# Where the SBUF tiles lie: both operands of every matrix product at whole multiples of 256 bytes

## The chip, the cores and the metric

The kernel runs on one core of one Trainium2 chip. What is measured is device time in microseconds (us) of one execution. The kernel before takes 1617.59 us (median of three runs, 1617.21 to 1617.77). The on-chip memory SBUF has 128 partitions; a tile has the same byte address in each of them, so "address" below means the byte within a partition.

## The reference

One layer of a decoder: a normalised input goes through one wide projection, then two token mixers run side by side (a three-branch attention and a retention), their outputs are gated and projected, and a two-matrix MLP follows. Sequence 1024, width 1024, MLP width 4096, all in float32. Cut to its skeleton:

```
h = rmsnorm(x)
q, kc, vc, ks, vs, kw, vw, gates, rq, rk, rv, rg, gate_a, gate_b = split(h @ w_in)
A = nsa_mixer(...)                 # compressed + selected + sliding-window attention
B = silu(rg) * retention(rq, rk, rv)
x = x + (sigmoid(gate_a) * (A @ w_proj_a) + sigmoid(gate_b) * (B @ w_proj_b)) @ w_out
x = x + square(relu(rmsnorm(x) @ w_up)) @ w_down
return rmsnorm(x)
```

## The kernel before

**How a float32 product is made.** TensorE multiplies a stationary operand (128 columns, loaded by a weight load, shown as PEld) by a moving operand of up to 512 columns that streams past it. A float32 value is split into a high part (`h`, made by a copy to float32r on ScalarE) and a low part (`l`, the difference, on VectorE). A product of two such values is three TensorE products: high by high, high by low, low by high, added up in PSUM. Every one of them goes through `mm` on line 157, so nearly all TensorE time stands on that line, and the tile names tell the products apart.

**Stages, in order of time.**

- 0 to 430 us, the wide projection and the retention. `bh`, `bl` (the two parts of the normalised, transposed input, 8 by 1024 columns) are stationary, 128 columns at a time; the weights `wh`, `wl` move, 512 columns (280 for `w_kvb`). `dense_tok` issues 24 products per token tile; every two inner steps it calls `tick`, which may put other work in between, and products of the retention and transposes stand between the token tiles.
- 430 to 790 us, attention. Scores are `QQ`, `ql` by `KKs`, `KKw`, `KKc`; probabilities are transposed and multiplied with `Vs`, `Vw`, `Vc`. Pieces of the gate products (`gps`: `wh`, `wl` stationary, `bh`, `bl` moving) are put between them, three products at a time.
- 790 to 880 us, the two mixer projections: `wh`, `wl` stationary, `Ah`, `Al`, `Bh`, `Bl` moving. The PSUM tile is shown as `mm` here too.
- 880 to 986 us, the output projection (`mmu`), 16 runs of 24 products with `bh`, `bl` stationary and the weights moving, and four transposes between the runs.
- 986 to 1302 us, the first MLP matrix (`mmu`): seven products of 12 for each of 16 weight groups (a Strassen-like scheme), `wh`, `wl` stationary, `bh`, `bl` or the forms `t2h` to `t4l` moving.
- 1302 to the end, the second MLP matrix (`mmd`): 1344 products whose two operands both come from the ring of split tiles `wh`, `wl`.

The order of TensorE's instructions is written out by hand for the whole program (`manual_schedule`, line 116); the order on the other engines follows from a scheduler with the pools' buffers.

**Where tiles lie.** A pool takes its place on a stack from the left end of SBUF or, with `side="right"`, on one from the right end, and gives it back when it closes. The tiles of a pool stand one behind the other, each rounded up to 32 bytes. In the built program the left stack begins at byte 16512 (128 past a multiple of 256), the right one ends at byte 229344 (224 past one). The first pool on the left, `cst`, holds the identity matrix (512 bytes) and five small tiles of 64, 32, 32, 64 and 32 bytes as rounded; 736 bytes in all, so that everything on the left behind it begins 96 past a multiple of 256, as far as the tiles between are multiples of 256 themselves. `cret` (2848 bytes), `cmp_m` (480 bytes), the four buffers each of `sums`, `mx` and `cf` (32 bytes each) shift what follows them further. On the right `big` (with `bh`, `bl`) ends at byte 229344. The remainders of the operands' first bytes by 256, out of the built programs of before and after:

| tiles | remainder before | after |
|---|---|---|
| `bh`, `bl`; `t2h` to `t4l`; `KKs`, `KKw`, `KKc`, `Vs`, `Vw`, `Vc`; `qt`, `qkT` | 224 | 0 |
| `wh`, `wl` in the pools `wring`, `wr4`, `wr5`, `wr7`; `Ah`, `Al`, `Bh`, `Bl`; `x1t` | 96 | 0 |
| `wh`, `wl` in `wrx` and `wr2`; the retention's `s`, `v`, `n`, `sd`; `ident` | 128 | 0 |
| `QQ`, `ql`, `pS`, `pW` | 64 | 0 |
| `ph`, `pl` | 192 | 0 |
| slices of `w_kvb` (280 columns, 1120 bytes apart) | 96, 128, 192, 224 | 0 |

All slices that are used as operands otherwise begin at multiples of 512 bytes within their tiles. Before, the products of the 790 to 880 us stage and of the last stage have both operands at 96; all other products with 512 moving columns have operands with two different remainders (224 with 96 or 128 or 64).

Of the kernel before, what the change touches and what calls it, by code (L numbers as in the profile page):

```python
# [9 lines left out]
F32 = mybir.dt.float32  # L10
F32R = mybir.dt.float32r
I32 = mybir.dt.int32
AF = mybir.ActivationFunctionType
OP = mybir.AluOpType
# [3 lines left out]
P = 128  # L18
S = 1024
D = 1024  # L20
NT = S // P
KD = D // P
# [90 lines left out]
def hybrid_block(ctx: ExitStack, tc: tile.TileContext, a: dict, out: bass.AP):  # L113
    nc = tc.nc
    V, A, G, T = nc.vector, nc.scalar, nc.gpsimd, nc.tensor
    ctx.enter_context(tc.manual_schedule(engines={mybir.EngineType.PE}))

    cst = ctx.enter_context(tc.tile_pool(name="cst", bufs=1, reuse_waits="tile"))
    dram = ctx.enter_context(tc.tile_pool(name="scr", bufs=1, space=DRAM))
    bigs = ctx.enter_context(ExitStack())  # L120
    big = bigs.enter_context(tc.tile_pool(name="big", bufs=1, side="right", reuse_waits="tile"))
    wraw = ctx.enter_context(tc.tile_pool(name="wraw", bufs=3, reuse_waits="tile"))
# [8 lines left out]

    bh = big.tile([P, KD, S], F32R, name="bh")
    bl = big.tile([P, KD, S], F32R, name="bl")
    ident = cst.tile([P, P], F32, name="ident")
    small = cst.tile([P, 16], F32, name="small")
    nhalf = cst.tile([P, 4], F32, name="nhalf")
    gcol = cst.tile([P, KD], F32, name="gcol")
    ssx = cst.tile([P, 2, NT], F32, name="ssx")
    rr = cst.tile([P, NT], F32, name="rr")
    V.memset(nhalf, -0.5)  # L140
    clock = {"t": 0, "n": 0}
    due = []
# [13 lines left out]
    def mm(o, w, m, start, stop):  # L156
        T.matmul(o, w, m, start=start, stop=stop)  # L157

    def load_raw(src, shape):
        r = wraw.tile([P, 1024], F32, name="raw", tag="raw")  # L160
        n = int(np.prod(shape))
        v = r[:, :n]
        if len(shape) == 2:
            v = v.rearrange("p (a b) -> p a b", a=shape[0])
        nc.sync.dma_start(v, src)
        return r[:, :n], n
# [6 lines left out]
    def new_slot(pool=None):  # L173
        if pool is None:
            pool = ring["pools"][ring["i"] % len(ring["pools"])]
            ring["i"] += 1
        h = pool.tile([P, 1024], F32R, name="wh", tag="wh")
        l = pool.tile([P, 1024], F32R, name="wl", tag="wl")
        return h, l

    def split_w(src, shape, eng=None, pool=None):
        r, n = load_raw(src, shape)
        h, l = new_slot(pool)
        A.activation(h[:, :n], r, AF.Copy)
        (eng or V).tensor_tensor(l[:, :n], r, h[:, :n], op=OP.subtract)  # L185
        return h, l
# [41 lines left out]
    def chunk_weights(name, n, s0=0, s1=4):  # L228
        per = 2
        W = []  # L230
        for s in range(s0, s1):
            h, l = split_w(a[name][:, s * per:(s + 1) * per, :], (per, n))
            for e in range(per):
                W.append((h[:, e * n:(e + 1) * n], l[:, e * n:(e + 1) * n]))
        return W

    with ExitStack() as es:
        psA = es.enter_context(tc.tile_pool(name="psA", bufs=2, space=PSUM, reuse_waits="tile"))
        tabs = es.enter_context(tc.tile_pool(name="tabs", bufs=1, reuse_waits="tile"))
        cret = tabs.tile([P, P + 512 + 72], F32, name="cret")  # L240
        cosr = tabs.tile([P, NT, 64], F32, name="cosr")
        sinr = tabs.tile([P, NT, 64], F32, name="sinr")
        cosn = tabs.tile([P, NT, 8], F32, name="cosn")
# [5 lines left out]
        with ExitStack() as e1:  # L249
# [150 lines left out]
            with tc.manual_schedule(engines={mybir.EngineType.PE, mybir.EngineType.Pool}):  # L400
# [9 lines left out]
                W = chunk_weights("w_r0a", 512, 0, 1)  # L410
# [24 lines left out]
            for c in range(2):  # L435
                rt = {}
                for j in range(NT):
# [21 lines left out]
                    if j == NT - 1:  # L459
                        W = chunk_weights(f"w_r{c}b", 512)  # L460
# [4 lines left out]
                for j in range(NT):  # L465
                    ps = psA.tile([P, 512], F32, name="mm", tag="mm")
                    dense_tok(ps, j, W, 0, 4)
                    if j == 0:
                        s = ret_s(0, qkT)
# [8 lines left out]
                    if j == NT - 1:  # L478
                        W = chunk_weights("w_kva" if c else "w_r1a", 512)
                    v, y = ret_v(j, ps)  # L480
                    cur = (j, c, qkT, s, v, y)
                    if j + 1 < NT:
                        qkT = qkTn
                        s = ret_s(j + 1, qkT)
# [32 lines left out]
        with ExitStack() as e2:  # L517
# [157 lines left out]
            for j in range(2, NT):  # L675
                ps = psA.tile([P, 512], F32, name="mm", tag="mm")
                dense_tok(ps, j, W)
                if j == NT - 1:
                    W = chunk_weights("w_kvb", 280)
                kva_post(j, ps)  # L680
            for j in range(NT):
# [5 lines left out]
                if j == NT - 1:  # L687
                    W = chunk_weights("w_q", 512)
                n = tmp.tile([P, 512], F32, name="n")[:, :256]
# [13 lines left out]
            for i, j in enumerate(reversed(range(NT))):  # L703
# [6 lines left out]
                n = tmp.tile([P, 512], F32, name="n")  # L710
# [56 lines left out]
    with ExitStack() as e3:  # L767
        msk = e3.enter_context(tc.tile_pool(name="msk", bufs=1, reuse_waits="tile"))
# [2 lines left out]
        psO = e3.enter_context(tc.tile_pool(name="psO", bufs=1, space=PSUM, reuse_waits="tile"))  # L771
        at = e3.enter_context(tc.tile_pool(name="at", bufs=2, reuse_waits="tile"))
        edge_m = msk.tile([P, 640], F32, name="edge_m")
        cmp_m = msk.tile([P, 120], F32, name="cmp_m")
        nc.sync.dma_start(edge_m, a["c_edge"])
        nc.sync.dma_start(cmp_m, a["c_cmp"])
        nc.sync.dma_start(gcol, a["norm_mlp"].rearrange("o (k p) -> p (o k)", p=P))
# [17 lines left out]
        def scores(qb, g, hp, u):  # L795
            QQ, ql = qs[qb, g]
            nk, nw = qb + 1, min(qb + 1, 5)
            cS, cW = nk * P, nw * P
            w0 = (nk - nw) * P
            u.update(nk=nk, nw=nw, P=[])  # L800

            def mask(c0, n, width, edge):
                if c0 + n == width:
                    return edge_m[:, 640 - n:]
                return edge_m[:, :n] if edge else edge_m[:, P:P + 1].to_broadcast([P, n])

            for i in range(2):
                h = hp * 2 + i
                sums = at.tile([P, 5], F32, name="sums", bufs=4)
                mx = at.tile([P, 5], F32, name="mx", bufs=4)  # L810
                pS = at.tile([P, 1024], F32, name="pS", bufs=PS_S)
                pW = at.tile([P, 768], F32, name="pW", bufs=PS_S)
                G.memset(pW[:, 704:], 0.0)
                for base, KK, start, width, p in ((1, KKs, 0, cS, pS), (2, KKw, w0, cW, pW)):
                    groups = []
                    for c0 in range(0, width, 512):
                        n = min(512, width - c0)
                        groups.append([(base if c0 == 0 else base + 2, KK, start + c0, n,
                                        mask(c0, n, width, base == 2), p[:, c0:c0 + n])])
                    split = len(groups) > 1  # L820
                    if base == 2:
                        tail = (0, KKc, 0, 64, cmp_m[:, 56 - 8 * qb:120 - 8 * qb], pW[:, 640:704])
                        if groups[-1][0][3] <= 448:
                            groups[-1].append(tail)
                        else:
                            groups.append([tail])
                    exps = []
                    for gi, grp in enumerate(groups):
                        ps = psS.tile([P, 512], F32, name="S")
                        off = 0  # L830
                        done = []
                        for b, K, c0, n, mk, o in grp:
                            done.append((b, ps[:, off:off + n], mk, o))
                            off += n
                        _, K, c0 = grp[0][:3]
                        mm(ps[:, :off], QQ[:, h], K[:, g, c0:c0 + off], True, False)
                        mm(ps[:, :off], ql[:, h], K[:, g, c0:c0 + off], False, True)
                        for b, sc, mk, o in done:
                            V.tensor_tensor_reduce(sc, sc, mk, -0.125, BIGPOS, OP.add, OP.min, mx[:, b:b + 1])  # L839
                            exps.append((b, sc, o))  # L840
                        if gi < len(groups) - 1:
                            yield
                    if split:
                        V.tensor_tensor(mx[:, base:base + 1], mx[:, base:base + 1], mx[:, base + 2:base + 3],
                                        op=OP.min)
                    for b, sc, o in exps:
                        m = b - 2 if b > 2 else b
                        A.activation(o, sc, AF.Exp, bias=mx[:, m:m + 1], scale=-1.0, accum_out=sums[:, b:b + 1])  # L848
                    if base == 1:
                        yield  # L850
                if cS > 512:
                    V.tensor_add(sums[:, 1:3], sums[:, 1:3], sums[:, 3:5])
                cf = at.tile([P, 3], F32, name="cf", bufs=4)
                V.reciprocal(cf, sums[:, :3])
                hd = g * 4 + hp * 2 + i
                V.tensor_mul(cf, cf, gts[:, qb, hd * 3:hd * 3 + 3])  # L856
                for b, v in ((1, pS[:, :cS]), (2, pW[:, :cW]), (0, pW[:, 640:704])):
                    G.tensor_scalar(v, v, cf[:, b:b + 1], 1.0, op0=OP.mult, op1=OP.mult)  # L858
                u["P"].append((pS, pW))
                yield  # L860
# [95 lines left out]
    with ExitStack() as e4:  # L956
# [40 lines left out]
        for i in range(8):  # L997
            h, l = pw[i]
# [56 lines left out]
    with ExitStack() as e5:  # L1055
# [40 lines left out]
        def up_first(X, ticks=False):  # L1096
            p1 = headp.tile([P, 512], F32, name="p1")
            A.activation(p1, prod(X[11], 11, ticks), AF.Copy)
            return {"p1": p1}
# [7 lines left out]
        with ExitStack() as e6:  # L1107
# [44 lines left out]
            W = out_w(0)  # L1152
            for c in range(2):
                cs = slice(c * 512, (c + 1) * 512)
                order = (0, 1, 4, 2, 5, 3, 6, 7) if c else range(NT)
                for n, j in enumerate(order):
# [4 lines left out]
                    if c == 0 and n == NT - 1:  # L1161
                        W = out_w(1)
# [71 lines left out]
        s = heads[0]  # L1234
        for p in range(16):
# [8 lines left out]
            if p < 15:  # L1244
                up_weights(p + 1, nra, nX)
                X = nX
                s = heads[1] if p == 0 else up_first(X)
# [90 lines left out]
    for step, n in enumerate((1, 2, 7, 6, 5, 4, 3)):  # L1338
# [12 lines left out]
        for i in range(4):  # L1351
            b = bank[i]
# [83 lines left out]
```

## Time and profile before

| | |
|---|---|
| median of three runs | 1617.59 us |
| the profiled execution, its own time | 1619.48 us |
| its span on the core | 1617.7 us |
| TensorE busy | 1576.0 us, 97% of the span, 7879 products |
| VectorE, ScalarE, GpSimd busy | 1070.7, 731.8, 436.5 us |
| mean granted TensorE clock | 0.991 |

The span is the time from the first to the last instruction that the hardware profiler saw. A product's duration in the trace runs from its start to its modelled end and is longer than its distance to the next product, since products are pipelined: of products that follow each other without a break, the distance from start to start is the *pace*, and it is the pace, not the duration, that adds up to time. A view of a window gives, for each engine, the time in which it was busy and the number of instructions that touch the window.

### The profile page before, as it was taken

Reading aid. Unit: us, or ns where it says so; the run is one execution under the profiler, and the core shown is the slowest. Engines: PE = TensorE matmul, PEld = TensorE weight load, DVE = VectorE, ACT = ScalarE, POOL = GpSimd, SP = SyncE. Lnnn points to the kernel's source line nnn. Section 1 sums busy time; section 2 is a strip of 40 time slices with the busy share of each in tenths; the row PEclk is TensorE's granted clock in tenths of the full one; section 3 lists DMA queues with packets and bytes.
Section 4 is the critical chain, followed back from the end, with each engine's and each line's share of the span. In section 5 each row is a group of like instructions: output and inputs, shape, how many; then the busy total and the mean of one; then the engine's idle time right before and its main releaser. Section 6 shows DMA issues by size and latency. Waiting matters only on the chain.

```text
span 1617.7 us, 22741 instructions
## 1 busy us (share of the span) xinstructions
PE 1576.0 (97%) x7879; PEld 1307.3 (81%) x7879; DVE 1070.7 (66%) x2170; ACT 731.8 (45%) x1627; POOL 436.5 (27%) x516
## 2 busy tenths in 40 slices
PE   7999999999999999999999998999999999999997
PEld 5888888887888888888788876888888878888886
DVE  4765564573777777776655367777667657885683
ACT  5454454573677766676522233222222234443442
POOL 4211010001232323333000013644555426621320
PEclk7999999999999999999999999999999999999999
DMA  6112101252111111121544322444444498674472
GB/s 213 50 36 66 52 18 43 66 182 67 49 47 34 53 46 53 47 60 60 182 144 156 109 94 74 160 144 145 152 153 150 160 332 286 207 230 126 132 269 101
DMA packets 98915, 191.83 MB, mean 119 GB/s; under 512 B 26928, under 2 KB 29360, under 8 KB 98800
## 3 DMA queue, kind: packets, MB, share of 16 engines
q1 hardware_dynamic: 98240, 188.55, 35.8%
q0 software_dynamic: 560, 1.84, 0.3%
q8 instruction: 62, 1.02, 0.3%
q14 instruction: 53, 0.43, 0.1%
HBM read 140.02 MB, written 50.33 MB: 118 GB/s over the span
## 4 chain that ended last, share of the span: by engine, by line
PE 83%; DVE 5%; ACT 4%; issue 3%; POOL 2%; DMA 2%; SPq 0%; POOLq 0%; ACTq 0%; DVEq 0%
PE mmu L157 23%; PE mm L157 20%; PE mmd L157 18%; PE gps L157 8%; PE S L157 4%; PE O L157 3%; PE pt L894 2%; PE pt L893 2%; ACT pW L848 1%; DVE S L839 1%; DVE pl L896 1%; PE pO L157 1%; PE pc L157 1%; ACT pS L848 1%; DVE wl L185 0%
## 5 line engine op out<-in xcount | busy, mean ns | idle before, releaser
L1030 DVE TENSOR_TENSOR wl<-raw,wh 128x1024 fp32r<-128x1024 f32 x121 | 182.8, 1535 | 68.5 <-ACT wh L1029 68.3
L1029 ACT ACTIVATE wh<-raw 128x1024 fp32r<-128x1024 f32 x121 | 125.2, 1056 | 217.8 <-PE mmd L157 131.3
L157 PE MATMUL mm<-wh,bh 128*128 128x512 f32 (+1 forms) x448 | 177.1, 395 | 1.0 <-ACT n L581 1.0
L157 PE MATMUL mm<-wh,bl 128*128 128x512 f32 (+1 forms) x448 | 172.7, 385 | 4.7 <-DVE bl L211 4.7
L157 PE MATMUL mmd<-wl,wh 128*128 128x512 f32 x448 | 174.6, 390 | 1.6 <-DVE wl L1030 1.6
L157 PE MATMUL mmd<-wh 128*128 128x512 f32 x448 | 174.5, 390 | 0.9 <-DVE u L1216 0.9
L157 PE MATMUL mmd<-wh,wl 128*128 128x512 f32 x448 | 174.5, 389 | 0.0
L157 PE MATMUL mm<-wl,bh 128*128 128x512 f32 (+1 forms) x448 | 172.1, 384 | 0.1
L896 DVE TENSOR_TENSOR pl<-pt,ph 128x512 fp32r<-128x512 f32 (+1 forms) x160 | 103.8, 649 | 30.2 <-ACT ph L895 27.8
L895 ACT ACTIVATE ph<-pt 128x512 fp32r<-128x512 f32 (+1 forms) x160 | 90.3, 567 | 55.0 <-PE pt L894 51.0
L839 DVE CUSTOM_DVE_ANT_0 S<-S,edge_m 128x512 f32<-128x512 f32 (+3 forms) x192 | 100.7, 530 | 14.7 <-PE S L157 12.7
L157 PE MATMUL gps<-bh,wh 128*128 128x512 f32 x256 | 108.5, 424 | 0.3 <-ACT gst L751 0.2
L858 POOL TENSOR_SCALAR pS<-pS,cf 128x1024 f32<-128x1024 f32 (+7 forms) x64 | 47.8, 748 | 220.2 <-DVE cf L856 71.4
L157 PEld LDWEIGHTS mm<-wh,bl 128*128 128x128 f32 x448 | 85.2, 190 | 22.9 <-DVE bl L211 5.7
L157 PE MATMUL mmu<-bh,wh 128*128 128x512 f32 x256 | 101.3, 396 | 0.0
L157 PE MATMUL mmu<-bl,wh 128*128 128x512 f32 x256 | 101.1, 395 | 0.0
L157 PE MATMUL mmu<-bh,wl 128*128 128x512 f32 x256 | 100.9, 394 | 0.0
L157 PE MATMUL gps<-bh,wl 128*128 128x512 f32 x256 | 100.9, 394 | 0.0
L157 PE MATMUL gps<-bl,wh 128*128 128x512 f32 x256 | 100.7, 393 | 0.0
L157 PEld LDWEIGHTS mmd<-wl,wh 128*128 128x128 f32 x448 | 84.1, 188 | 19.4 <-DVE wl L1030 2.0
L157 PEld LDWEIGHTS mmd<-wh 128*128 128x128 f32 x448 | 84.1, 188 | 18.5 <-issue 1.3
L157 PEld LDWEIGHTS mmd<-wh,wl 128*128 128x128 f32 x448 | 84.1, 188 | 17.5
(312 smaller groups left out, 3975.3 us busy)
## 6 DMA issues: line engine op xcount, KB each, us to landing
raw<-u_scr SPq DMA_DIRECT2D x56, 512.0 KB, 3.9
raw<-w_down SPq DMA_DIRECT2D x41, 512.0 KB, 4.7
raw<-w_up SPq DMA_DIRECT2D x32, 512.0 KB, 3.6
u_scr<-u SPq DMA_DIRECT2D x60, 256.0 KB, 2.3
u_scr<-s SPq DMA_DIRECT2D x45, 256.0 KB, 2.1
y<-w_down SPq DMA_DIRECT2D x16, 512.0 KB, 6.7
x<-x SPq DMA_DIRECT2D x8, 512.0 KB, 3.9
qt<-q_scr SPq DMA_DIRECT2D x32, 128.0 KB, 2.5
```

Source lines behind the costliest of these rows:

```text
L157: T.matmul(o, w, m, start=start, stop=stop)
L839: V.tensor_tensor_reduce(sc, sc, mk, -0.125, BIGPOS, OP.add, OP.min, mx[:, b:b + 1])
L848: A.activation(o, sc, AF.Exp, bias=mx[:, m:m + 1], scale=-1.0, accum_out=sums[:, b:b + 1])
L858: G.tensor_scalar(v, v, cf[:, b:b + 1], 1.0, op0=OP.mult, op1=OP.mult)
L893: T.transpose(tp[:, bi * 2], p0, ident)
L894: T.transpose(tp[:, bi * 2 + 1], p1, ident)
L895: A.activation(ph[:, :n], tp[:, :n], AF.Copy)
L896: V.tensor_sub(pl[:, :n], tp[:, :n], ph[:, :n])
L1029: A.activation(h[:, :n], r, AF.Copy)
L1030: V.tensor_sub(l[:, :n], r, h[:, :n])
```

## The change

It moves tiles to other places; it adds, removes and reorders no instruction. The built program has the same instructions in the same order on all five engines as before; the forms differ in one place, the four loads of `w_kvb` and their splits, which are now written as two rows of 280 with 512 columns from one to the next (before: 560 in one piece). The waits differ in two places, both on VectorE: the first use of `sums` no longer waits for a DMA, and a wait for VectorE itself is added to the first split of the mixer projections.

- `small`, `gcol`, `rr` (128 bytes as rounded) go into a pool `few` ahead of `cst` on the left: 16512 + 128 = 16640 = 65 x 256. `nhalf`, `ssx` and the four `sums` (224 bytes) go to the right end, ahead of `big`: 229344 - 224 = 229120 = 895 x 256.
- `cret` and `cmp_m` are allocated wider, and the part that was there before is used. `cf` moves ahead of `pS`, so that `mx` and `cf` together take 256 bytes.
- `chunk_weights` splits its loads itself, each row of a slot at its own half (2048 bytes apart).

```diff
@@ -115,6 +115,9 @@
+    few = ctx.enter_context(tc.tile_pool(name="few", bufs=1, reuse_waits="tile"))
+    few2 = ctx.enter_context(tc.tile_pool(name="few2", bufs=1, side="right", reuse_waits="tile"))
+    smp = ctx.enter_context(tc.tile_pool(name="smp", bufs=4, side="right", reuse_waits="tile"))
     cst = ctx.enter_context(tc.tile_pool(name="cst", bufs=1, reuse_waits="tile"))
@@ -131,12 +134,12 @@
     bh = big.tile([P, KD, S], F32R, name="bh")
     bl = big.tile([P, KD, S], F32R, name="bl")
+    small = few.tile([P, 16], F32, name="small")
+    gcol = few.tile([P, KD], F32, name="gcol")
+    rr = few.tile([P, NT], F32, name="rr")
+    nhalf = few2.tile([P, 4], F32, name="nhalf")
+    ssx = few2.tile([P, 2, NT], F32, name="ssx")
     ident = cst.tile([P, P], F32, name="ident")
-    small = cst.tile([P, 16], F32, name="small")
-    nhalf = cst.tile([P, 4], F32, name="nhalf")
-    gcol = cst.tile([P, KD], F32, name="gcol")
-    ssx = cst.tile([P, 2, NT], F32, name="ssx")
-    rr = cst.tile([P, NT], F32, name="rr")
@@ -229,15 +232,19 @@
         for s in range(s0, s1):
-            h, l = split_w(a[name][:, s * per:(s + 1) * per, :], (per, n))
+            r = wraw.tile([P, 1024], F32, name="raw", tag="raw")
+            r, h, l = (t.rearrange("p (a b) -> p a b", a=per)[:, :, :n] for t in (r, *new_slot()))
+            nc.sync.dma_start(r, a[name][:, s * per:(s + 1) * per, :])
+            A.activation(h, r, AF.Copy)
+            V.tensor_tensor(l, r, h, op=OP.subtract)
             for e in range(per):
-                W.append((h[:, e * n:(e + 1) * n], l[:, e * n:(e + 1) * n]))
+                W.append((h[:, e], l[:, e]))
@@
-        cret = tabs.tile([P, P + 512 + 72], F32, name="cret")
+        cret = tabs.tile([P, 6 * P], F32, name="cret")[:, :P + 512 + 72]
@@ -771,7 +778,7 @@
-        cmp_m = msk.tile([P, 120], F32, name="cmp_m")
+        cmp_m = msk.tile([P, P], F32, name="cmp_m")[:, :120]
@@ -806,8 +813,9 @@
-                sums = at.tile([P, 5], F32, name="sums", bufs=4)
+                sums = smp.tile([P, 5], F32, name="sums")
                 mx = at.tile([P, 5], F32, name="mx", bufs=4)
+                cf = at.tile([P, 3], F32, name="cf", bufs=4)
@@ -850,7 +858,6 @@
-                cf = at.tile([P, 3], F32, name="cf", bufs=4)
```

## The prediction

> **What bounds the kernel now.** The first part of the page, the slices and the waits of TensorE:
>
> ```profile
> span 1617.7 us, 22741 instructions
> PE 1576.0 (97%) x7879; PEld 1307.3 (81%) x7879; DVE 1070.7 (66%) x2170; ACT 731.8 (45%) x1627; POOL 436.5 (27%) x516
> PEclk7999999999999999999999999999999999999999
> ...
> PE mm L157 <- DVE bl L211: 4.7, 1, 4.7
> PE tp L1119 <- DVE x1t L1163: 4.6, 3, 1.9
> PE pt L894 <- POOL pS L858: 4.3, 7, 1.8
> PE mmu L157 <- ACT wh L1029: 4.1, 1, 4.1
> ```
>
> TensorE is busy for all but 42 us, its longest waits are under 5 us each, and its clock is granted in full after the first slice. Nothing else sets the end: the time is the number of products times their pace. A change of places can only pay through the pace, so that is what I read next, in three windows in which TensorE does nothing but products with 512 moving columns (the columns are the window's ends, its length, then busy time and number for TensorE, the weight loads, VectorE, ScalarE and GpSimd, the clock, and the DMA engines' share and rate):
>
> ```profile
> 805.00:865.00 60.00, 60.00 (x266) 49.74 (x265) 35.67 (x51) 12.38 (x17) 0.00 (x0) 1.00 0.48 150
> 1100.00:1280.00 180.00, 180.00 (x776) 146.12 (x775) 127.50 (x150) 40.30 (x46) 87.41 (x63) 1.00 0.44 149
> 1320.00:1580.00 260.00, 260.00 (x1149) 215.40 (x1148) 190.40 (x155) 110.70 (x132) 94.63 (x40) 1.00 0.67 216
> ```
>
> About two of the counted products reach over a window's ends. The last window (`mmd`, both operands at remainder 96) makes 260 / 1147 = 226.7 ns for each; the first (mixer projections, also 96 and 96) 60 / 264 = 227.3; the middle one (first MLP matrix, 224 against 96) 180 / 774 = 232.6. Same shape, same full clock, and TensorE never idle in any of them: the middle one is 5.9 ns slower a product. The other engines are no explanation: the last window has more VectorE time a microsecond (0.73 against 0.71), more ScalarE (0.43 against 0.22) and more DMA (0.67 against 0.44), and is the faster one. The durations say the same by tile, rows of the groups in the last two windows:
>
> ```profile
> L157 PE MATMUL mmd<-wh,wl 128*128 128x512 f32 x383 | 149.2, 389 | 0.0
> ...
> L157 PE MATMUL mmu<-bl,wh 128*128 128x512 f32 x147 | 58.1, 395 | 0.0
> L157 PE MATMUL mmu<-t4h,wh 128*128 128x512 f32 x40 | 15.8, 396 | 0.0
> ```
>
> How the two paces come about is seen in starts (first column, us), first in the middle window, then where the projections begin:
>
> ```profile
> 1101.14 0.40 PE L157 MATMUL mmu<-t4l,wh 128*128 128x512 f32 x1
> 1101.38 0.41 PE L157 MATMUL mmu<-t4h,wl 128*128 128x512 f32 x1
> 1101.62 0.40 PE L157 MATMUL mmu<-t4h,wh 128*128 128x512 f32 x1
> 1101.85 0.39 PE L157 MATMUL mmu<-t4l,wh 128*128 128x512 f32 x1
> 1102.08 0.39 PE L157 MATMUL mmu<-t4h,wl 128*128 128x512 f32 x1
> 1102.31 0.39 PE L157 MATMUL mmu<-t4h,wh 128*128 128x512 f32 x1
> 1102.54 0.39 PE L157 MATMUL mmu<-t4l,wh 128*128 128x512 f32 x1
> 1102.77 0.40 PE L157 MATMUL mmu<-t4h,wl 128*128 128x512 f32 x1
> 1103.00 0.41 PE L157 MATMUL mmu<-t4h,wh 128*128 128x512 f32 x1
> ...
> 792.67 0.40 PE L157 MATMUL mm<-Bh,wl 128*128 128x512 f32 x1
> ...
> 795.00 0.39 PE L157 MATMUL mm<-Ah,wh 128*128 128x512 f32 x1
> 795.22 0.39 PE L157 MATMUL mm<-Al,wh 128*128 128x512 f32 x1
> 795.45 0.39 PE L157 MATMUL mm<-Ah,wl 128*128 128x512 f32 x1
> 795.67 0.39 PE L157 MATMUL mm<-Ah,wh 128*128 128x512 f32 x1
> 795.90 0.39 PE L157 MATMUL mm<-Al,wh 128*128 128x512 f32 x1
> ```
>
> In the middle window the long product (0.41) comes back every sixth; that pattern runs on from one product group to the next, over tiles at other addresses. In the projections the ten products after the start take 2.33 us, 233 ns each, and then the pace settles at 225 to 227 and stays. I read this as two streams out of SBUF, the moving operand and the next weights, that get in each other's way depending on their relative place: with equal remainders the pair finds a steady state at 226.7 ns, with different ones it wanders through six, at 232.6 ns on average. This is an inference from addresses and paces; no row names the cause.
>
> **The change part by part.** Instructions, order and queues stay as they are, so nothing is added and nothing removed. What changes is the pair of remainders, for every product, to 0 and 0. The 384 products of the projections and the 1344 `mmd` products had equal remainders already and keep their pace: 0. For the others with 512 columns the price is 232.6 - 226.7 = 5.9 ns, once settled, and nothing for the first ten after a break, as the start of the projections shows. The chain of waits gives the lengths of unbroken rows (start, us, products):
>
> ```profile
> 51.39 5.58 PE mm L157 x24
> 90.52 2.86 PE mm L157 x12
> 149.36 24.49 PE mm L157 x106
> 314.76 3.10 PE mm L157 x24
> 889.93 5.57 PE mmu L157 x24
> 999.40 299.47 PE mmu L157 x1282
> ```
>
> - First MLP matrix: 1282 in one row, 1282 x 5.9 = 7.6 us.
> - Output projection: 16 runs of 24, broken by four transposes each time, 14 settled products in a run: 16 x 14 x 5.9 = 1.3 us.
> - Wide projection: 1152 products with 512 columns. 384 of them stand in runs of 12 (like 90.52): nothing. The rest are 32 runs of 24, some joined (the row of 106), some with retention or compression products inside. If all were clean, 32 x 14 x 5.9 = 2.6; I take 2.0.
> - Attention: 768 gate products, three at a time between others, and 176 score products in pairs: nothing settles, 0.
> - Products with 128 to 280 columns: 0, for the same reason; the 192 of `w_kvb` (the row of 314.76, 3.10 / 24 = 129 ns) could at most gain the same 2.5%, 0.6 of 24.8 us.
>
> Sum 10.9 us, say 11. From below: a pair at 0 and 0 need not settle, and then it is 0. From above: if every different pair gained at once, 3824 products (1152, 384, 1344, 768, 176) x 5.9 = 22.6 us.
>
> The edits that could cost something: `w_kvb` now lands in rows of 1120 bytes, half as long, four loads:
>
> ```profile
> raw<-w_kvb SPq DMA_DIRECT2D x4, 280.0 KB, 3.1
> L165 SPq DMA_DIRECT2D raw<-w_kvb x4: 328/333/333, 244.1 to 251.4; - x4
> 298.82 0.38 PE L157 MATMUL mm<-wh,bh 128*128 128x280 f32 x1
> ```
>
> They go out at 244 to 251 and the first product is at 298.8: were the 3.1 us doubled, more than 40 us would still cover them; without that cover it would be 3 us once. The splits keep their number of elements. The added wait on VectorE is for its own earlier work. Faster products ask more of the others only by 2.5%; in the middle window VectorE is free for 52 of 180 us and ScalarE for 140, and there they wait for TensorE, not it for them:
>
> ```profile
> ACT wh L1029 <- PE mmu L157: 123.5, 37, 4.8
> ```
>
> The wait of 4.1 us before the first MLP matrix stays, since what it waits for runs behind TensorE's last output products; VectorE's work there is as long as before.
>
> The Trainium skill speaks against all of it: "TensorE: Matmul & The Clock Gate", Part 2, says that loading the next weights takes no SBUF bandwidth from the running product, and "SBUF — State Buffer", "Who interferes with whom", that TensorE never waits on anyone; by them places would not matter and the sum would be 0 (the rival "nothing" below). The trace disagrees as far as it goes, with 226.7 and 232.6 ns for one shape at one clock.
>
> **The sum.** Span 1617.7 - 11 = 1606.7; the profiled execution's own time, 1619.48, lies 1.8 us above its span and 1.9 above the median of the runs. I forecast runs of 1617.6 - 11 = 1606.6 us.
>
> **The rivals.**
>
> *More than the difference.* Equal remainders of 96 may be a half-good place, and starting on the boundary may free the settled pace too. For: the only products with 512 columns of two-byte elements in the trace, the warm-up, last 379 ns at the least, 10 less than `mmd`'s 389, so there is a faster pace to be had at this clock.
>
> ```profile
> L157 PE MATMUL mm<-warm x17: 379/634/635, 1.2 to 7.0; 128*128 128x512 bf16 x17
> ```
>
> Against: those read half the bytes and lie at remainder 160, and products moving from 128 are no faster than those moving from 96. If the unbroken rows got it (1344 + 384 + 1282 + 224 of the output projection + 340 of the wide one, 3574 x 10 = 36) on top of the 11: 1570 us; for all 5552 and with the upper bound of 22.6 it would be 1539. By the Trainium skill, the same page, "Back-to-back issue gap", the estimate of a warm pace is 512 / 2.4 + 2.5 = 215.8 ns; that is 10.9 under `mmd`.
>
> *Nothing.* Where the remainders are equal, both operands also lie in the left half of SBUF, while everywhere else one is on the left and one on the right. If that distance is what counts, the change moves nothing across: 1617.6 us. For: no row with 512 columns separates the two. Against: the settling after a start looks like a matter of phase.
>
> *Slower: a lock in the wrong place.* The steady state of 0 and 0 is a new one. If both reads starting on a boundary hold each other up at the worst step of the six (0.24 us, 1101.38 to 1101.62), all unbroken rows take 241 ns: 1282 + 224 + 340 products lose 8.4 ns, 1728 lose 14.3, 40 us together: 1658 us. It decides from a settled pace p at which the gain of about 1840 products is eaten by 1728: 1840 x (232.6 - p) = 1728 x (p - 226.7), p = 229.7 ns. Against it: the one equal pair in the trace settles at the low end of the six.
>
> **How the numbers follow.** My forecast (1598 to 1611 by itself) has 0.55, more than the difference 0.22, nothing 0.14, slower 0.09. About 0.2%, 3.2 us, is what a measurement of this kernel can tell from no change. So faster 0.77, within it 0.14, slower 0.09. The range from 1578 to 1618.5 takes in the forecast, the case of nothing and half of the faster rival; what it leaves out is the other half, 0.11, and the slower case.
>
> **What would show it.** Right: `mmu` with moving `bh`, `bl` and `t4h` at 389 instead of 394 to 396; the chain's row of 1282 products at 291 us instead of 299.5; `mmd` unchanged at 389; gate products hardly moved; VectorE's sums the same. Wrong: `mmd` below 385 (the first rival), `mmu` still at 395 (the second), `mmd` above 392 (the third), or a new wait of TensorE over 5 us.

## The result, and the profile after

| | before | after |
|---|---|---|
| median of 4 runs each | 1617.4 us (1615.4 to 1617.8) | 1605.0 us (1604.1 to 1606.1) |
| ratio, with its 95% interval | | 0.9926 (0.9909 to 0.9943) |
| the profiled execution, its span | 1617.7 us | 1602.3 us |

The kernel is 12.4 us faster. The forecast was 1606.6. The first part of the page of the kernel after, the clock by slices, and the longest waits of TensorE:

```profile
span 1602.3 us, 22741 instructions
PE 1557.7 (97%) x7879; PEld 1301.9 (81%) x7879; DVE 1069.8 (67%) x2170; ACT 731.6 (46%) x1627; POOL 435.1 (27%) x516
PEclk8999999999999999999999999999999999999999
```

```profile
PE mm L160 <- DVE bl L214: 5.2, 1, 5.2
PE tp L1126 <- DVE x1t L1170: 4.8, 3, 2.0
PE pt L901 <- POOL pS L865: 4.5, 7, 1.8
PE mmu L160 <- ACT wh L1036: 4.2, 1, 4.2
```

TensorE's busy time fell by 18.3 us with the same 7879 products; the other engines did the same work in the same time (VectorE 1069.8 us against 1070.7). The long waits are the old ones: the one of 5.2 us stands where 4.7 stood before. How much of the 18.3 us is the pace, and where a part of it went into waits, is worked out below by stages. The same three windows, moved 5, 10 and 10 us ahead because the work comes earlier (the columns as in the prediction):

```profile
800.00:860.00 60.00, 60.00 (x266) 49.71 (x265) 35.45 (x50) 12.44 (x17) 0.00 (x0) 1.00 0.45 149
1090.00:1270.00 180.00, 180.00 (x795) 149.02 (x794) 132.94 (x155) 41.45 (x47) 88.51 (x64) 1.00 0.43 152
1310.00:1570.00 260.00, 260.00 (x1149) 215.36 (x1148) 188.10 (x156) 110.64 (x132) 93.62 (x40) 1.00 0.65 214
```

Two of the counted products again reach over the ends. The first MLP matrix now makes 180 / 793 = 227.0 ns a product (232.6 before), the mixer projections 60 / 264 = 227.3 and the third layer 260 / 1147 = 226.7, both as before. The starts in the middle window show the round with one long step gone (first column the start, us); every product now follows at 0.22 or 0.23:

```profile
1094.80 0.39 PE L160 MATMUL mmu<-bl,wh 128*128 128x512 f32 x1
1095.02 0.39 PE L160 MATMUL mmu<-bh,wl 128*128 128x512 f32 x1
1095.25 0.39 PE L160 MATMUL mmu<-bh,wh 128*128 128x512 f32 x1
1095.48 0.39 PE L160 MATMUL mmu<-bl,wh 128*128 128x512 f32 x1
1095.70 0.39 PE L160 MATMUL mmu<-bh,wl 128*128 128x512 f32 x1
```

By groups (busy us, mean ns of one):

```profile
L160 PE MATMUL mmd<-wl,wh 128*128 128x512 f32 x448 | 174.4, 389 | 1.6 <-DVE wl L1037 1.6
L160 PE MATMUL gps<-bh,wh 128*128 128x512 f32 x256 | 108.2, 423 | 0.3 <-ACT gst L758 0.2
L160 PE MATMUL mmu<-bh,wh 128*128 128x512 f32 x256 | 99.7, 389 | 0.0
```

`mmu` from `bh` is at 389 instead of 394 to 396, `mmd` stayed at 389, and the first gate product went from 424 to 423.

**Where the 15.4 us of the two spans lie.** The chain of waits has the start of each stage (start, us, products). First of the kernel before, the rows that the prediction didn't show, then of the kernel after:

```profile
37.08 3.40 issue
...
385.56 5.59 PE gps L157 x24
...
792.33 87.39 PE mm L157 x383
879.72 9.77 PE mmu L157 x42
...
958.29 5.51 PE mmu L157 x17
...
1310.26 291.13 PE mmd L157 x1283
```

```profile
33.90 3.37 issue
48.21 5.47 PE mm L160 x24
...
145.40 23.86 PE mm L160 x106
...
379.58 5.46 PE gps L160 x24
785.77 88.72 PE mm L160 x383
874.49 9.54 PE mmu L160 x42
...
890.40 5.48 PE mmu L160 x24
...
951.82 3.91 PE mmu L160 x17
...
991.16 292.41 PE mmu L160 x1282
...
1294.89 291.14 PE mmd L160 x1283
```

| stage (start of its first row to the next) | before | after | difference | predicted |
|---|---|---|---|---|
| start of the program | 37.1 | 33.9 | -3.2 | 0 |
| wide projection, retention, compression | 348.5 | 345.7 | -2.8 | -2.0 |
| attention | 406.8 | 406.2 | -0.6 | 0 |
| mixer projections | 87.4 | 88.7 | +1.3 | 0 |
| output projection | 119.7 | 116.7 | -3.0 | -1.3 |
| first MLP matrix | 310.9 | 303.7 | -7.1 | -7.6 |
| from the third layer to the end | 307.4 | 307.4 | 0.0 | 0 |

The row of 1282 begins after the first 50 products of the first MLP matrix and the row of 1283 after the first 25 of the third layer; these count to the line before.

Three of these differences are, all but a few tenths, not the change's. The first 3.2 us lie in the program's start, where products of the wide projection run at half clock in both executions, with starts 0.43 us apart up to 29.5 us before and up to 25.0 after. How long the start takes differs between kernels with the same places too: the row that begins at 37.08 here begins at 34.43 and 35.51 in two kernels below that leave this stage as it was before (the kernel before with 64 and with 32 columns). The 1.3 us and about 1.6 of the 3.0 are stretches of TensorE at half its clock, which fell in different places in the two profiled executions. In the kernel after there is one at the start of the projections (a window view of TensorE alone: busy time and products, granted clock, DMA share and rate; then two starts in it):

```profile
786.90:789.90 3.00, 3.00 (x8) 0.50 1.01 329
```

```profile
786.94 0.63 PE L160 MATMUL mm<-Bh,wl 128*128 128x512 f32 x1
787.37 0.63 PE L160 MATMUL mm<-Bh,wh 128*128 128x512 f32 x1
```

In the kernel before the same stretch ran at full clock, but the row of 17 output products at 958.29 took 5.51 us, with starts 0.43 us apart, where the kernel after takes 3.91 at 951.82. Those two cancel in part. Without these accidents the stages give -2.8 - 0.6 - 1.4 - 7.1 = -11.9 us, beside the medians' -12.4.

The products themselves gained more than that. The wide projection's stage before and after (TensorE alone: busy time and products, granted clock, DMA share and rate), and the wait that grew most in it (us in total, times, the longest):

```profile
37.08:385.56 348.48, 346.13 (x1856) 1.00 0.20 64
33.90:379.58 345.68, 342.07 (x1856) 1.00 0.20 65
```

```profile
PE pS L157 <- DVE qkT L317: 0.2, 1, 0.2
PE pS L160 <- DVE qkT L324: 1.3, 2, 1.0
```

TensorE worked 4.1 us less there, but sat idle 3.6 us instead of 2.4 (3.2 to 3.6 in three executions with equal remainders, 2.4 to 2.7 in three with the places of before), so 2.8 us arrived. In attention its work shrank by 1.3 us and its idle time grew by 0.7. Of the 18.3 us, then, 4.2 lie in the program's start, 0.3 in the half-clock stretches and 13.8 in the pace, and 2.0 of these went into longer waits.

### The profile page after: what moved, and what is told of

Read it like the earlier page. It is cut to its first block, busy times and chain, and to the rows that moved or that the text cites. A ratio compares the mean times of both kernels' runs of the same rounds, so it can differ in the third digit from the quotient of the medians.

```text
span 1602.3 us, 22741 instructions
## 1 busy us (share of the span) xinstructions
PE 1557.7 (97%) x7879; PEld 1301.9 (81%) x7879; DVE 1069.8 (67%) x2170; ACT 731.6 (46%) x1627; POOL 435.1 (27%) x516
## 4 chain that ended last, share of the span: by engine, by line
PE 84%; DVE 5%; ACT 4%; issue 3%; POOL 2%; DMA 2%; SPq 0%; POOLq 0%; ACTq 0%; DVEq 0%
PE mmu L160 23%; PE mm L160 20%; PE mmd L160 18%; PE gps L160 8%; PE S L160 4%; PE O L160 3%; PE pt L901 2%; PE pt L900 2%; ACT pW L856 1%; DVE S L847 1%; PE pO L160 1%; PE pc L160 1%; DVE pl L903 1%; ACT pS L856 1%; DMA y<-w_down 0%
```

## The experiments

The theory on trial: the pace of long products (those with 512 moving columns) depends on where the moving operand lies *relative* to the stationary one, modulo 256 bytes; equal remainders lock at 226.7 ns. Three others could give the same result: that the boundary of 256 bytes itself is what pays; that the side of SBUF or the distance counts; and that it is one of two pairs, a product's own operands or the moving one and the *next* product's weights, which are loaded while it runs. In the window rows below, all of TensorE alone, the pace is the length divided by the number less two, as before. The runs of the kernel before beside the first four kernels had a median of 1617.2 us.

### All remainders 128 instead of 0

```diff
-    few = ctx.enter_context(tc.tile_pool(name="few", bufs=1, reuse_waits="tile"))
+    few = ctx.enter_context(tc.tile_pool(name="few", bufs=1, side="right", reuse_waits="tile"))
```

With `few` (128 bytes) on the right too, the left pools start 128 bytes before the boundary and the right ones as well, so both operands of every product are 128 past a multiple of 256.

> The changed kernel with the 128 bytes of small tiles on the left moved to the right end too: every operand of every product now begins 128 past a multiple of 256, so all remainders are equal but none is 0. Theory A (only the difference of the two operands' remainders counts): as the changed kernel, 1605 us, products of the first MLP matrix at 389 ns in the trace. Theory B (starting on the 256-byte boundary counts): back to 1615 to 1618 us, mmu at 394 to 396 ns.

Measured: 1602.1 us, 0.9905 of before (0.9888 to 0.9921).

```profile
1090.00:1270.00 180.00, 180.00 (x796) 1.00 0.44 151
1310.00:1570.00 260.00, 260.00 (x1149) 1.00 0.64 212
```

180 / 794 and 260 / 1147 are both 226.7 ns. Whole multiples of 256 bytes are not needed; no operand lies on one here. 1602.1 is 3 us under the changed kernel; so both were run again beside each other, with 11 runs of before (median 1616.9). The changed kernel:

> The changed kernel once more, beside the one with all remainders at 128 (few narrow tiles moved to the right end too). If the boundary of 256 bytes itself counts for nothing, the two agree within 0.2% (3 us): this one 1604 to 1606 us. If all-128 is truly better, it stays about 2 to 3 us above it.

All at 128:

> Both operands of every product 128 bytes past a multiple of 256. Place counts only as a difference: 1602 to 1606 us, within 0.2% of the changed kernel in the same runs, since the paces of its stages agree with the changed kernel's to 0.1 ns and its one look was shorter by one pause of 2 us at the first products of the third layer. All-128 better in itself: 1601 to 1603 us, and under the changed kernel by 2 us or more.

Measured: 1604.6 us, 0.9921 (0.9908 to 0.9935), and 1603.8 us, 0.9913 (0.9897 to 0.9929). The intervals overlap over most of their length: the two can't be told apart, and the 3 us were the spread of runs.

### Left at 224, 192 and 160, right at 0

Three kernels that shift only the left pools, by the number of bytes of narrow tiles ahead of them:

```diff
-    small = few.tile([P, 16], F32, name="small")
-    gcol = few.tile([P, KD], F32, name="gcol")
-    rr = few.tile([P, NT], F32, name="rr")
+    gcol = few.tile([P, 24], F32, name="gcol")[:, :KD]
...
+    rr = ssx[:, 0]
...
-        cret = tabs.tile([P, 6 * P], F32, name="cret")[:, :P + 512 + 72]
+        cret = tabs.tile([P, 6 * P], F32, name="cret")
+        small = cret[:, P + 512 + 72:P + 512 + 88]
+        cret = cret[:, :P + 512 + 72]
```

That is the one at 224; `gcol` of 16 columns gives 192, of `KD` columns 160. The first MLP matrix and the gates (moving on the right) then differ by 32, 64 and 96 bytes, the wide and the output projection (moving on the left) by 224, 192 and 160. The mixer projections and the third layer have both operands on the left and stay equal. At 224:

> The changed kernel with everything on the left 32 bytes lower (remainder 224), the right side left at 0: differences of 32 where the right side moves (mmu, gps) and of 224 where the left side moves (mm), mmd and the mixer projections equal as always. Theory A: any difference costs as before, 1615 to 1618 us, mmu at 394 to 396 ns, mmd at 389. If only whole 64- or 128-byte pieces counted (32 is less than one): 1605 us. Theory B: between the two, since bh and bl still begin on the boundary.

At 192:

> As the last, with the left side 64 bytes lower (remainder 192): differences of 64 and 192. Theory A: 1615 to 1618 us, mmu at 394 to 396 ns. If the time grows with the difference, more than the kernel with 32. If one of these differences were a better place than 0, mmu or mm below 389 and the time below 1605 us.

At 160:

> The kernel of the change with all small tiles so placed that the left pools start 160 bytes past a multiple of 256 and the right ones at 0: the moving operand lies 96 bytes past the stationary one in the second MLP layer and the transposes of the output projection's input (96), and 160 in the wide projection; the third layer (left against left) stays equal. Of the differences placed so far 32, 128, 192 and 224 bytes ran at 232.5 to 233.5 ns a product and 64 at 228.9. If what counts is the difference in units of 64 bytes and 64 is a lucky one, 96 is no whole number of 64 and runs at about 233 (the whole kernel about 1618 us, 3824 long products or fewer at 6 ns); if the pace falls smoothly with the distance from 64, 96 runs between 229 and 233, some 231 (about 1615 us). The projection at 160 stays at 233 by both.

Measured at 224: 1619.3 us, 1.0010 (1.0000 to 1.0019).

```profile
1090.00:1270.00 180.00, 180.00 (x773) 1.00 0.43 145
1310.00:1570.00 260.00, 260.00 (x1149) 1.00 0.66 221
```

At 192: 1613.8 us, 0.9975 (0.9965 to 0.9984).

```profile
1090.00:1270.00 180.00, 180.00 (x788) 1.00 0.45 152
1310.00:1570.00 260.00, 260.00 (x1149) 1.00 0.67 218
```

At 160: one run, 1620.6 us, beside 1616.6 of before.

```profile
1090.00:1270.00 180.00, 180.00 (x773) 1.00 0.43 145
1310.00:1570.00 260.00, 260.00 (x1149) 1.00 0.67 221
```

A shift of 32 bytes takes the whole gain away (the time is 1.3 us above theory A's range): 180 / 771 = 233.5 ns in the first MLP matrix, while the third layer, whose operands moved together, keeps 260 / 1147 = 226.7 in all three. That is the theory's own test: nothing but the relative place was undone, and only the stages where it was undone slowed. In the first MLP matrix it was the stationary operand alone that moved, and that operand is read by its weight load: so the load is a party to what sets the pace. A difference of 64 bytes is the exception, 180 / 786 = 229.0, and its starts come in a round of three (226, 229, 232 ns). 96 is back at 233.5, so of the two forms expected for it, "only a lucky 64" is right and a smooth fall with the distance is not. Each difference has a round of its own in the first MLP matrix: seven steps at 128 bytes, four at 32 (235, 234, 234, 231 ns), three at 96 (238, 231, 231). Taking the mean distance of starts over the long products of a stage from the eleventh after a break on (distances under 260 ns):

| moving less stationary, modulo 256 | 0 | 32 | 64 | 96 | 128 | 160 | 192 | 224 |
|---|---|---|---|---|---|---|---|---|
| pace, ns | 226.7 | 233.3 | 228.9 | 233.3 | 232.4 | 234.3 | 233.3 | 233.3 |
| stage | first MLP | first MLP | first MLP | first MLP | first MLP, before | wide projection | wide projection | wide projection |

### Low halves 128 bytes from high halves

Every operand is split into a high and a low half, and a group of three products is high with high, high with low, low with high. Here all low halves lie at remainder 128 and all high ones at 0, by pads and pools of their own (two small scratch tiles give up a buffer for the room):

```diff
+        lp = stack.enter_context(tc.tile_pool(name=name + "l", bufs=bufs, reuse_waits="tile"))
+        stack.enter_context(tc.tile_pool(name=name + "b", bufs=1, reuse_waits="tile")).tile([P, 32], F32, name=name + "pb")
...
-        l = pool.tile([P, 1024], F32R, name="wl", tag="wl")
+        l = lows.get(id(pool), pool).tile([P, 1024], F32R, name="wl", tag="wl")
...
-    bl = big.tile([P, KD, S], F32R, name="bl")
+    bl = bigl.tile([P, KD, S], F32R, name="bl")
```

A product's own operands then differ in two of three products. In the order in which they run, the weights loaded for the next product always have the remainder of the operand that is moving.

> The changed kernel with the low part of every split operand 128 bytes off the boundary (wl, bl, Al, Bl, t2l to t4l), the high parts on it. In a triple of products (high by high, high by low, low by high) two of the three then have operands with different remainders, but the weights that are loaded while a product runs (those of the next one) always have the remainder of the operand that is moving. Theory A1 (moving operand against the weights loaded meanwhile): no loss, 1605 us, mmu and mmd at 389 ns. Theory A2 (a product's own two operands): two of three products disturbed everywhere, mmd too: mmu and mmd at 393 to 395 ns, 1617 us and 6 to 8 us more for mmd and the projections, 1623 to 1626 us. Theory B: low parts off the boundary, some loss, 1609 to 1615 us.

Measured: 1619.4 us, 1.0013 (1.0004 to 1.0023).

```profile
800.00:860.00 60.00, 60.00 (x261) 1.00 0.46 146
1090.00:1270.00 180.00, 180.00 (x781) 1.00 0.44 151
1310.00:1570.00 260.00, 260.00 (x1127) 1.00 0.65 214
```

The time lies in none of the three ranges. The paces are 231.7, 231.1 and 231.1 ns. The third layer, which had never moved from 226.7 in any kernel so far, lost 4.4 ns with both operands on the left as ever: the side and the distance are out, and so is the next weights' place as the only thing that counts, since that was equal throughout. A product's own pair alone is out too: products with equal operands ran at 230.1 in the third layer, those with moving high and stationary low at 230.0, those with moving low and stationary high at 233.3. An equal pair between unequal ones does not keep 226.7; it takes a row in which all lie alike.

This kernel also tells the period 256 from 512, which the others can't: wherever a settled row has equal remainders by 256 in them, the built programs have equal ones by 512 too. Here the starts come in a round of six (224, 232, 226, 236, 235, 234 ns in the third layer), and it runs on unchanged whether the moving operand and the next weights lie at equal places by 512 or 256 apart: 43 rounds in which all six pairs are equal took 231.1 ns a product, 39 in which all are 256 apart took 231.1 as well.

### A shorter weight load

Does the load of the weights take part at all? Here the stationary operand is cut to its first 64 columns in all products of the first MLP matrix and of the third layer but the first and the last of each sum; half of the contributions to the output's rows is left out there. The moving operand keeps its 512 columns. The edit in the first MLP matrix, made alike in the third layer, in the kernel after and in the kernel before:

```diff
-                mm(ps, h[:, ks], yl, False, False)
+                mm(ps[:64], h[:, kc], yl, False, False)
```

After, with 64 columns:

> The changed kernel with the stationary operand cut to its first 64 of 128 columns in all but the first and last product of each sum in the second and third MLP layers: it leaves out half of the output rows' contributions there, and half of what each weight load reads, while the moving operand's 512 columns stay. Theory L, the weight load of the next product shares something with the running product's reads (each load costs a few ns of the pace, and more where the remainders differ): the pace falls from 226.7 ns to about 221, and with 2900 such products the kernel becomes some 10 to 17 us faster than the changed kernel, 1588 to 1595 us. Theory S, the pace is set by the moving operand's own stream against the stationary operand's place, whatever the load's length: 226.7 stays within 0.3 ns, and the time within 1603 to 1607 us.

Before, with 64 columns:

> The kernel before with the same cut of the stationary operand to 64 columns in the second and third MLP layers. Theory L: the loss of 5.9 ns a product in the second layer (232.5 against 226.7) is caused by the weight load, so half a load gives about half of the loss: 229 to 230 where the remainders differ and 226.7 or less where they are equal, and the kernel takes 1606 to 1613 us. Theory S: the second layer keeps 232.5 and the third 226.7, and the kernel 1616 to 1619 us.

Measured: 1611.2 us and 1618.5 us, one run each, beside 1616.6 of before. The windows of the changed kernel with the cut, then of the kernel before with it:

```profile
1090.00:1270.00 180.00, 180.00 (x787) 1.00 0.44 152
1310.00:1570.00 260.00, 260.00 (x1132) 1.00 0.65 213
```

```profile
1090.00:1270.00 180.00, 180.00 (x783) 1.00 0.44 151
1310.00:1570.00 260.00, 260.00 (x1132) 1.00 0.65 215
```

Neither theory holds. With half the weight load the equal pairs got *slower*, 229.3 and 230.1 ns against 227.0 and 226.7, and the unequal one faster, 180 / 781 = 230.5 against 232.6. The time of the second kernel, 1618.5, is just what theory S asked for; the windows show that it is a gain in one stage and a loss in the other. What the four paces share is that the place hardly matters any more (1.2 ns in the first MLP matrix, where it was 5.6). That was put to the test with 32 columns (`ps[:32]`, `k * P + 32`), after and before:

> The changed kernel with the stationary operand cut to 32 columns in all but the first and last product of each sum in the second and third layers (three quarters of the contributions of the output rows are left out there). With 64 columns both layers slowed from 226.7 to 229.5 to 230 ns. Theory P, only a full load beside a full stream locks, and any shorter load runs in the same round of six at about 230 wherever the operands lie: 229 to 231. Theory Q, the pace follows the load's length: with equal remainders it goes further up, to 232 or 233.

> The kernel before with the same cut to 32 columns. With 64 columns its second layer (remainders 224 and 96) came down from 232.5 to 230.3 ns and its third (96 and 96) went up from 226.7 to 230. Theory P: both near 230, and within 1 ns of the changed kernel's. Theory Q: the second layer further down, to 228, and the third further up, to 232 or 233.

Measured: 1614.1 us and 1624.3 us, one run each, beside 1616.9 of before. The windows of the changed kernel with 32 columns, then of the kernel before:

```profile
1090.00:1270.00 180.00, 180.00 (x781) 1.00 0.43 151
1310.00:1570.00 260.00, 260.00 (x1125) 1.00 0.64 210
```

```profile
1090.00:1270.00 180.00, 180.00 (x780) 1.00 0.43 148
1310.00:1570.00 260.00, 260.00 (x1125) 1.00 0.65 213
```

The paces are 231.1 and 231.5 after, 231.4 and 231.5 before: a little above theory P's 229 to 231, and equal wherever the operands lie; theory Q's 228 for the unequal pair is not there, nor its 232 for the equal one. So the place of the operands pays only together with a stationary operand of all 128 columns. Two reservations: the cut also halves the rows that a product writes, which these runs don't separate from the load, and the small step from 230 to 231.3 between 64 and 32 columns is not explained.

The Trainium skill has it otherwise: "TensorE: Matmul & The Clock Gate", Part 2, "Step-by-step: what each phase is for", says that loading the next tile's weights "doesn't steal SBUF read bandwidth from the running matmul". If so, neither the place nor the length of the load should move the pace of an unchanged moving stream. Moving the stationary operand alone by 32 bytes moved it from 226.7 to 233.3 ns, and halving it by +3.4 ns in the third layer and -2.1 in the kernel before's first MLP matrix. The measurements decide that the load matters here; whether it is read bandwidth that the two share, they don't show.

## Why the prediction was right, and where not

- **Only the pace can pay.** Right: the same products, no new long wait, and 13.8 us less work of TensorE from the pace. But what paid was less, 11.9 us: the faster products of the wide projection and of attention waited 2.0 us longer for the other engines, which the sum left out because they ask only 2.5% more of them.
- **Which stages.** Right, by undoing it: the shift of 32 bytes put the first MLP matrix back to 233.5 ns and left the third layer at 226.7.
- **First MLP matrix, 7.6 us.** Measured 7.1. The pace fell by 5.65 ns in the mean of all its unbroken products (232.38 to 226.73), 7.2 us over 1282; the 5.9 came from a window with a pace of 232.6.
- **Output projection, 1.3 us.** Measured 1.4 once the half-clock stretch is taken off, some 5.59 to 5.49 us a run of 24.
- **Wide projection, 2.0 us.** Mis-sized: 2.8. A run of 24 went from 5.58 to 5.47, 0.11 us and not 14 x 5.9 = 0.08, and the joined row of 106 from 24.49 to 23.86. The step that failed is "nothing for the first ten after a break", taken from one start in the projections. In the wide projection the mean of the first ten distances fell from 232.8 to 230.5 ns. The start in the projections was a slow one: its ten steps (241, 234, 233, 236, 224, 231, 236, 229, 232, 231 ns, then 226 to 227) are one series, and other restarts of equal rows enter it later. Of 21 rows of 16 or more in the wide projection of the kernel after, nine ran through nine or ten such steps, six through three to six, and six through the last two alone. The products there gained 4.1 us in all, of which the waits took 1.3. `w_kvb` gained 0.03 us a run (3.10 to 3.07), well inside the bound of 0.6.
- **Attention, 0.** Nearly: 0.6 us. The gate products' mean fell from 233.0 to 231.9 ns. Three at a time settle no row, but not all stand so: an unbroken row of 24 at the start of the stage (5.59 to 5.46 us) and one of 36 at its end gained 0.33 us, which the sum left out.
- **The split of `w_kvb` costs nothing.** Right as far as the trace shows: no wait of TensorE for it appeared.
- **The reason.** Half right. "Relative place" was the right variable and the steady state of equal remainders the right picture. The pair that was named, the moving operand and the *next* weights, is not it alone: with that pair always equal the row ran at 231.1 ns. The round was misread: in the kernel before's first MLP matrix the long step comes back every seventh product (185 of 187 times), as the starts 1101.38 and 1103.00 already show, and not every sixth; the sum does not hang on it. What a row needs to lock is known only as a condition (all remainders alike, full load), not as a mechanism.
- **The rivals.** *More than the difference*: `mmd` stayed at 389 and 226.7 ns, and at 0, 96, 128, 160, 192 and 224, each time with both operands alike, the third layer never ran faster; the boundary has nothing to give. *Nothing*: the first MLP matrix has its operands on opposite sides still and runs at 226.7. *Slower*: the settled pace of 0 and 0 is 226.7, far under the 229.7 from which that case decided.

The sum of 10.9 stands against 11.9 by stages and 12.4 by the medians: the short rows gave 1.5 us more than was said, after their longer waits, the long one 0.5 less. That the total came so near is partly luck, since these misses cancel in part.

## What to carry to other kernels

Where TensorE is the bound and its long products run without a break, look at the distance from start to start, not at durations: a recurring round of longer and shorter steps at full clock was worth 2.5% of those products here, and it was removed by placing tiles so that both operands, high and low halves too, have the same address modulo 256 bytes. This is shown for float32 products of 128 by 128 with 512 moving columns; shorter ones were not tried apart. The common remainder did not matter among the six that were tried, so padding one side by the difference should do; a single 32-byte tile ahead of a pool can undo it. Faster products pay in full only where the other engines keep up. And a total that fits a theory is no proof: with 64 columns one stage won what the other lost, and only the paces by stage told so.

## What the hardware showed that was not expected

- A difference of 64 bytes costs 2.2 ns a product, in the same stage where 32 and 96 cost 6.6; but 192, its mirror image, costs 6.6 in the settled products of the wide projection.
- Fewer weights can make a product slower: 64 of 128 columns took the third layer from 226.7 to 230.1 ns.
- Where both operands moved together nothing changed: the third layer's 1283 products took 291.13 us before and 291.14 after.
- Short stretches at a granted clock of 0.50 follow some pauses of TensorE and not others, between executions of one kernel too, and the two that differed cost 1.3 and 1.6 us. In them starts are 0.43 us apart. Both agree with the Trainium skill, "TensorE: Matmul & The Clock Gate", Part 1, which gives 426.7 ns for 512 columns in the cold state and calls the window that decides it free-running.
